# A two-layer hybrid trunk: branch A's norm writes each tile in one piece into places of its own, and the first head's preparation is begun ten steps sooner

## The chip, the cores and the metric

The kernel runs on one core of one Trainium2 chip. Its time is the device time of one execution in microseconds. Five engines work side by side: TensorE (PE; its weight loads are listed as PEld), VectorE (DVE), ScalarE (ACT), GpSimd (POOL) and SyncE (SP). SyncE issues every DMA of this kernel, in the order of its one instruction stream. Each engine works through its own instructions in order and waits where an instruction needs another engine's result or a buffer that is not free yet.

## The reference

Two layers of a decoder trunk on 1024 positions of width 1024. In each layer an RMS norm, one combined input product, three token mixers, a gated sum of their projections, an output product and a residual. The parts that the change touches are the norm of mixer A and the first head of mixer B:

```
a = a_val * sigmoid(a_glu)
a = causal_dwconv(a, a_dw) + a_dw_b            # 31 taps, 512 channels
a = layernorm(a, a_ln_g, a_ln_b)
y_a = silu(a) * silu(a_z)
...
q, k, v = split(silu(causal_dwconv(qkv, b_conv)))  # 8 heads of 128
kk = einsum("bhnid,bhnjd->bhnij", k, k)            # chunks of 64
a_mat = eye(c) + beta * kk * gamma_strict
sol = triangular_solve(a_mat, [v*beta, k*beta*exp(gc)], lower, unit_diagonal)
```

## The kernel before, in words

In a layer the products with the input weights come in two stages. In the first, blocks of weights are taken in pairs: seven products for eight (the names A11, S2, A12, S1, S3, A22, S4 are the seven weight operands of a pair, A and S in the rows). Each of the seven has four steps of three matmuls 128x512 (L357), so a pair has 28 steps. A product is summed in one of four PSUM buffers `ps`; ScalarE copies it out (L369) or VectorE adds it to the outputs (L373, L376). Weights (`wr`, L223) are combined on POOL and split in two parts on ScalarE and POOL (L184, L185). The outputs `o` are q, k, v (with a short convolution: start L715, taps L695 on VectorE, end L717), gates `g` (activation L726) and others, stored to DRAM by L729. In the second stage (L281, then L257) single products run, and beside them the eight heads of mixer B, one after the other.

Side work is woven into the first stage by step numbers counted from the start of a pair: `interleave` runs a side generator's next piece at step so and so, with a gap. The table of such numbers stands at lines 41 to 48; `S_HEAD = -4, 1` puts the first head's preparation four steps ahead of the third-last pair. TensorE's and VectorE's orders follow the code as written; a scheduler lays out ScalarE, POOL and SyncE, by priorities and readiness.

Two side generators matter here.

*The norm of mixer A* (`a_norm`, L1087 to L1102). The convolution's result lies in four units `acc`, one per 128 channels, channels on partitions. For each of eight tiles of 128 positions, `to_norm` transposes four 128x128 blocks into one PSUM buffer `pa` (L1115), takes mean and variance (`ln_stats`: VectorE L1076, L1078, L1080, POOL L1082 for the power, VectorE L1084), and writes the normalised tile back over the four blocks in `acc` by four activations 128x128 (L1118). Two rounds later the same four blocks are transposed again into a `pa` (L1097) and four activations apply gain, offset and Silu (L1100). There are two `pa` buffers.

*The first head* (`first_head`, L1403): load of k, q and the decay exponents (L736, L753: `gam`), the decay matrix (`head_decay`: select on POOL L789, exponentials on ScalarE L794), the keys (transposes L762, copies L777 and sums of squares L780, L891), the products of keys and queries (L811, L830, on VectorE L812 to L833), then small 16x16 blocks of the triangular matrix, which go to DRAM and come back regrouped (L847, L852), a solve on VectorE in 15 steps (`head_sub`: L862, L864, L865), its result stored in four pieces (L872) and fetched regrouped (L879), and later, with the second head under way, the inverse (`head_inv`: VectorE transpose L918, TensorE L923, L930). The second head's preparation follows at the end of the first stage (`S_NEXT`, `second_head`); its decay load is an L753 too.

The units are 4 KB tiles per partition in a ring of 24; `U(name)` takes one and `F` gives it back.

Of the kernel before, what the change touches and what calls it, by code (L numbers as in the profile page):

```python
# [11 lines left out]
AF = mybir.ActivationFunctionType  # L12
# [3 lines left out]
P = 128  # L16
T = 1024
D = 1024
NT = 8
# [24 lines left out]
S_C_MIX = 14, 6  # L44
S_SCALARS = 5, 12
S_A_NORM = 8, 5
S_HEAD = -4, 1
S_NEXT = 50, 61, 77, 76, 74
STEP_US, IDLE_US, WIDE_US = 0.7, 1.5, 1.4
EXTRA = 2  # L50
# [20 lines left out]
def hybrid_trunk_kernel(ctx: ExitStack, tc: tile.TileContext, x, norm_g, w_in, a_dw, a_dw_b,  # L71
# [4 lines left out]
    pe, act, pool, sp = nc.tensor, nc.scalar, nc.gpsimd, nc.sync  # L76
# [28 lines left out]
    def U(name, dt=F32):  # L105
        ring = free.popleft()
        t = ring.tile([P, 1024], dt, name=name)
        held[id(t)] = (ring, t)
        return t

    def F(*ts):
        for t in ts:
            free.append(held.pop(id(t))[0])
# [16 lines left out]
    ident = const.tile([P, P], F32, name="ident")  # L130
# [618 lines left out]
    def head_load(s, names):  # L749
        for nm in names:  # L750
            if nm == "d":
                s.gam = U("gam")
                sp.dma_start(out=by_chunk(s.gam), in_=gc_d[:, s.hd, :].partition_broadcast(P))  # L753
                continue
            assert nm == "z" or (s.layer, "qkv".index(nm) * 8 + s.hd) in saved
            s.u[nm] = fetch({"k": k_d, "q": q_d, "v": v_d, "z": z_d}[nm][s.hd], nm + "T")
        yield
# [7 lines left out]
    hsl = [slice(h * HALF, (h + 1) * HALF) for h in range(2)]  # L765
# [308 lines left out]
    def ln_stats(tp):  # L1074
        bs = sm.tile([P, 6], F32, name="bs")
        dve.bn_stats(bs, tp)  # L1076
        mv = sm.tile([P, 2], F32, name="mv")
        dve.bn_aggr(mv, bs)  # L1078
        ve = sm.tile([P, 1], F32, name="ve")
        dve.tensor_scalar(out=ve, in0=mv[:, 1:2], scalar1=EPS, scalar2=None, op0=ALU.add)  # L1080
        rs = sm.tile([P, 1], F32, name="lrs")
        pool.tensor_tensor(out=rs, in0=ve, in1=mhalf[:, 0:1], op=ALU.pow)  # L1082
        nm = sm.tile([P, 1], F32, name="nm")
        dve.scalar_tensor_tensor(out=nm, in0=mv[:, 0:1], scalar=-1.0, in1=rs, op0=ALU.mult, op1=ALU.mult)  # L1084
        return rs, nm

    def a_norm(l, accs):  # L1087


        for t in range(NT + 2):  # L1090
            if t < NT:
                to_norm(accs, t)
            if t >= 2:
                ts = slice((t - 2) * P, (t - 1) * P)
                tb = pa.tile([P, HALF], F32, name="pa")
                for c in range(4):
                    pe.transpose(tb[:, c * P:(c + 1) * P], accs[c][:, ts], ident)  # L1097
                for c in range(4):
                    gc, b_ = cols["alg", l] + c, cols["alb", l] + c
                    act.activation(out=accs[c][:, ts], in_=tb[:, c * P:(c + 1) * P], func=AF.Silu,  # L1100
                                   scale=vec[:, gc:gc + 1], bias=vec[:, b_:b_ + 1])
            yield  # L1102

    def split_units(src, name):
# [2 lines left out]
        F(src)  # L1107
        return hi, lo

    def to_norm(us, t):  # L1110

        ts = slice(t * P, (t + 1) * P)
        tp = pa.tile([P, HALF], F32, name="pa")
        for c in range(4):
            pe.transpose(tp[:, c * P:(c + 1) * P], us[c][:, ts], ident)  # L1115
        rs, nm = ln_stats(tp)
        for c in range(4):
            act.activation(out=us[c][:, ts], in_=tp[:, c * P:(c + 1) * P], func=AF.Identity, scale=rs, bias=nm)  # L1118

    def c_norm(gvs):  # L1120
        for t in range(NT):
            to_norm(gvs, t)
            yield
# [167 lines left out]
    def layer(l, before, ws=None, parts=1):  # L1291
# [131 lines left out]
        def at_step(nm, d, gap):  # L1423
            return at[nm] * 28 + d, gap
# [5 lines left out]
                    (late(lambda: gate_scalars(l, r)), *at_step("scalars", *S_SCALARS)),  # L1430
                    (late(fetch_a), *at_step("a_norm", 0, 1)),
                    (late(lambda: a_norm(l, accs)), *at_step("a_norm", *S_A_NORM)),
                    (late(first_head), *at_step("head", *S_HEAD)),
                    (late(lambda: head_load(hs[1], "k")), *at_step("head", S_NEXT[0], 1)),
# [98 lines left out]
    def late(f):  # L1533
        yield from f()
# [73 lines left out]
```

## Time and profile before

| | |
|---|---|
| median of 3 runs | 2663.96 us (2663.27 to 2668.45) |
| profiled execution | 2663.31 us, of it a span of 2661.5 us |
| mean granted TensorE clock | 0.991 |
| busy TensorE / VectorE / ScalarE / POOL | 2568.4 / 1656.7 / 1256.4 / 1423.5 us |

The profile is of one execution. [...] "Wait" is the idle time in front of an instruction with the event that ended it. Layer 0's norm of mixer A lies at 520 to 570 us, its first head's solve at 678 to 694 us; the same places of layer 1 are some 1312 us later.

### The profile page before, as it was taken

The numbers are of one execution on the slowest core, as the hardware profiler recorded it, in microseconds if no ns is written. First come the engines' busy times: TensorE is split into PE (matmuls) and PEld (weight loads), VectorE is DVE, ScalarE is ACT, GpSimd is POOL, SyncE is SP. The second block draws the span as 40 slices with busy tenths as digits, with TensorE's granted clock in tenths as the row PEclk, the third lists the DMA queues.
The fourth block names the chain that finished last, engine by engine and source line by source line (L and its number), as shares of the span: only waits on it lengthen the run. The fifth ranks groups of instructions, "written<-read, shape, count | busy, mean of one in ns | idle before, by whom it ended". The sixth has DMA issues, their size and how long they took to land.

```text
span 2661.5 us, 42685 instructions
## 1 busy us (share of the span) xinstructions
PE 2568.4 (97%) x15963; PEld 2113.4 (79%) x15963; DVE 1656.7 (62%) x2934; ACT 1256.4 (47%) x2996; POOL 1423.5 (53%) x1144
## 2 busy tenths in 40 slices
PE   7899999999899999999999999999998999999998
PEld 6688888778688888788867888887787888877887
DVE  6698999756445454445276889997564545444442
ACT  4434434565466666322134343356554666652221
POOL 7867777768433332363167777776673333324520
PEclk9999999999999999999999999999999999999999
DMA  4122333534634445554312223343445444445432
GB/s 158 48 64 88 104 95 107 155 108 122 184 103 111 145 106 169 182 170 138 107 68 63 63 82 110 95 150 104 118 131 173 114 131 112 136 139 189 156 130 76
DMA packets 361636, 319.65 MB, mean 120 GB/s; under 512 B 98931, under 2 KB 313557, under 8 KB 360405
## 3 DMA queue, kind: packets, MB, share of 16 engines
q1 hardware_dynamic: 361428, 316.92, 39.5%
q8 instruction: 126, 2.06, 0.3%
q14 instruction: 82, 0.66, 0.1%
HBM read 221.12 MB, written 95.75 MB: 119 GB/s over the span
## 4 chain that ended last, share of the span: by engine, by line
PE 80%; DVE 6%; POOL 4%; ACT 4%; DMA 3%; issue 2%; SPq 0%; DVEq 0%; POOLq 0%; ACTq 0%
PE ps L357 36%; PE ps L257 24%; PE ps L1271 7%; DMA gam<-gc_d 2%; PE pa L762 1%; PE ps L281 1%; POOL S L185 1%; PE pr L1012 1%; PE pr L1004 1%; PE pr L995 1%; POOL st L298 1%; PE pr L1021 1%; DMA wr<-in_w_in_dram 1%; PE pa L811 1%; DVE nm L1084 1%
## 5 line engine op out<-in xcount | busy, mean ns | idle before, releaser
L185 POOL TENSOR_TENSOR S<-st,S 128x512 fp32r<-128x512 f32 x248 | 332.5, 1341 | 166.1 <-ACT S L184 165.7
L695 DVE SCALAR_TENSOR_TENSOR pr<-o,dwT,pr 128x512 f32<-128x512 f32 (+7 forms) x480 | 357.0, 745 | 10.6
L357 PE MATMUL ps<-hT,A 128*128 128x512 f32 x1488 | 363.5, 392 | 0.0
L185 POOL TENSOR_TENSOR wl<-wr,wh 128x512 fp32r<-128x512 f32 (+2 forms) x164 | 198.6, 1225 | 293.1 <-PE ps L257 138.7
L257 PE MATMUL ps<-hT,wh 128*128 128x512 f32 x960 | 334.4, 429 | 0.0
L373 DVE TENSOR_TENSOR o<-o,ps 128x512 f32<-128x512 f32 x430 | 286.2, 681 | 77.4 <-PE ps L357 66.2
L357 PEld LDWEIGHTS ps<-hT,A 128*128 128x128 f32 x1488 | 279.4, 189 | 58.5 <-issue 0.5
L184 ACT ACTIVATE S<-st 128x512 fp32r<-128x512 f32 x248 | 156.7, 632 | 338.3 <-PE ps L357 196.4
L185 POOL TENSOR_TENSOR A<-wr,A 128x512 fp32r<-128x512 f32 x186 | 253.0, 1361 | 22.3 <-ACT A L184 22.0
L695 DVE SCALAR_TENSOR_TENSOR pr<-o,cvT,pr 128x512 f32<-128x512 f32 (+3 forms) x288 | 213.1, 752 | 48.9 <-ACT pr L715 43.3
L257 PE MATMUL ps<-hT,wl 128*128 128x512 f32 x480 | 189.3, 394 | 0.0
L184 ACT ACTIVATE A<-wr 128x512 fp32r<-128x512 f32 x186 | 117.2, 630 | 143.6 <-PE ps L357 126.3
L357 PE MATMUL ps<-T,A 128*128 128x512 f32 x744 | 183.4, 393 | 0.9 <-POOL A L185 0.5
L357 PE MATMUL ps<-hT,S 128*128 128x512 f32 x744 | 183.7, 392 | 0.0
L357 PE MATMUL ps<-T2h,S 128*128 128x512 f32 x496 | 167.9, 396 | 5.7 <-ACT T2h L184 3.0
L357 PE MATMUL ps<-T3h,S 128*128 128x512 f32 x496 | 167.1, 395 | 4.1 <-ACT o L369 3.6
L357 PE MATMUL ps<-T1h,S 128*128 128x512 f32 x496 | 164.7, 391 | 0.0
L357 PEld LDWEIGHTS ps<-T,A 128*128 128x128 f32 x744 | 139.1, 189 | 31.3 <-ACT o L717 1.6
L184 ACT ACTIVATE wh<-wr 128x512 fp32r<-128x512 f32 (+2 forms) x164 | 85.6, 549 | 165.2 <-issue 123.5
L357 PEld LDWEIGHTS ps<-hT,S 128*128 128x128 f32 x744 | 138.1, 188 | 28.4 <-ACT o L717 0.7
L257 PEld LDWEIGHTS ps<-hT,wh 128*128 128x128 f32 x960 | 151.1, 190 | 11.6
L1271 PE MATMUL ps<-woh,mg 128*128 128x512 f32 x512 | 140.7, 391 | 0.0
(298 smaller groups left out, 5723.6 us busy)
## 6 DMA issues: line engine op xcount, KB each, us to landing
wr<-in_w_in_dram SPq DMA_DIRECT2D x160, 512.0 KB
g_d<-gth SPq DMA_DIRECT2D x32, 512.0 KB
g_d<-o SPq DMA_DIRECT2D x16, 512.0 KB
z_d<-o SPq DMA_DIRECT2D x16, 512.0 KB
v_d<-o SPq DMA_DIRECT2D x16, 512.0 KB
k_d<-o SPq DMA_DIRECT2D x16, 512.0 KB
q_d<-o SPq DMA_DIRECT2D x16, 512.0 KB
gam<-gc_d SPq DMA_DIRECT2D x16, 512.0 KB
```

The source lines that it names most:

```text
L184: act.activation(out=hi, in_=src, func=AF.Copy)
L185: lo_eng.tensor_tensor(out=lo, in0=src, in1=hi.bitcast(F32), op=ALU.subtract)
L257: pe.matmul(ps[h], lhsT=w[wi][:, k, :], rhs=rhs(h, ri, k), start=(k == 0 and i == 0), stop=(k == kt - 1 and i == 2))
L281: pe.matmul(ps[h][:, sl], lhsT=w[wi][:, k, :], rhs=rhs(h, ri, k)[:, sl], start=(k == 0 and i == 0), stop=(k == kt - 1 and i == 2))
L298: eng.tensor_tensor(out=out, in0=in0, in1=in1, op=ALU.subtract)
L357: pe.matmul(ps, lhsT=wt[:, wi, k, :], rhs=blk(nb, ri, k), start=(k == 0 and i == 0), stop=(k == 3 and i == 2))
L373: dve.tensor_tensor(out=out, in0=other, in1=ps, op=ALU.add)
L695: dve.scalar_tensor_tensor(out=acc[:, lo:], in0=x[:, h * HALF + lo - s:(h + 1) * HALF - s], scalar=taps[s - 1], in1=acc[:, lo:], op0=ALU.m ...
L762: pe.transpose(tp[:, j * P:(j + 1) * P], src[:, half * 4 + j, :], ident)
L811: pe.matmul(tp[:, j], lhsT=kT[:, n], rhs=qT[:, n], start=True, stop=True)
L995: pe.matmul(ks, lhsT=kT[:, n], rhs=st, start=True, stop=True)
L1271: pe.matmul(ps[h], lhsT=mg[hh, ri, k // 4][:, k % 4, off:off + P], rhs=wo[k][wi][:, h * HALF:(h + 1) * HALF], start=(k == 0 and i == 0), s ...
```

## The change

In `a_norm` two units `an` are taken; each is cut in two halves, which gives four places of 128 positions by 512 channels. `to_norm` writes tile t by one activation 128x512 into place t mod 4, and the second transposes read that place. Mixer C's norm calls `to_norm` without a place and keeps its four activations. `S_HEAD` goes from −4 to −14. In the changed kernel the new activation is L1122, the second transposes are L1099, the Silu is L1102, and lines behind are shifted.

```diff
--- before.py
+++ after.py
@@ -44,7 +44,7 @@
 S_C_MIX = 14, 6
 S_SCALARS = 5, 12
 S_A_NORM = 8, 5
-S_HEAD = -4, 1
+S_HEAD = -14, 1
 S_NEXT = 50, 61, 77, 76, 74
 STEP_US, IDLE_US, WIDE_US = 0.7, 1.5, 1.4
 EXTRA = 2
@@ -1087,18 +1087,22 @@
     def a_norm(l, accs):
 
 
+        both_ways = U("an"), U("an")
+        place = [u[:, sl] for sl in hsl for u in both_ways]
         for t in range(NT + 2):
             if t < NT:
-                to_norm(accs, t)
+                to_norm(accs, t, place[t % 4])
             if t >= 2:
                 ts = slice((t - 2) * P, (t - 1) * P)
                 tb = pa.tile([P, HALF], F32, name="pa")
                 for c in range(4):
-                    pe.transpose(tb[:, c * P:(c + 1) * P], accs[c][:, ts], ident)
+                    pe.transpose(tb[:, c * P:(c + 1) * P], place[(t - 2) % 4][:, c * P:(c + 1) * P], ident)
                 for c in range(4):
                     gc, b_ = cols["alg", l] + c, cols["alb", l] + c
                     act.activation(out=accs[c][:, ts], in_=tb[:, c * P:(c + 1) * P], func=AF.Silu,
                                    scale=vec[:, gc:gc + 1], bias=vec[:, b_:b_ + 1])
+            if t == NT + 1:
+                F(*both_ways)
             yield
 
     def split_units(src, name):
@@ -1107,13 +1111,16 @@
         F(src)
         return hi, lo
 
-    def to_norm(us, t):
+    def to_norm(us, t, place=None):
 
         ts = slice(t * P, (t + 1) * P)
         tp = pa.tile([P, HALF], F32, name="pa")
         for c in range(4):
             pe.transpose(tp[:, c * P:(c + 1) * P], us[c][:, ts], ident)
         rs, nm = ln_stats(tp)
+        if place is not None:
+            act.activation(out=place, in_=tp, func=AF.Identity, scale=rs, bias=nm)
+            return
         for c in range(4):
             act.activation(out=us[c][:, ts], in_=tp[:, c * P:(c + 1) * P], func=AF.Identity, scale=rs, bias=nm)
```

On ScalarE, at the first tiles of the norm in layer 0 (`an` is the new place, S and A are weight splits, `o` and `pr` a convolution). Before:

```order
L184 ACTIVATE S_4581<-st 128x512
L1118 ACTIVATE acc<-pa,nm,lrs 128x128 x8
L717 ACTIVATE o_4281<-pr 128x512
L1100 ACTIVATE acc<-pa,vec 128x128 x4
L184 ACTIVATE A_4631<-wr 128x512
L1118 ACTIVATE acc<-pa,nm,lrs 128x128 x4
L184 ACTIVATE S_4677<-st 128x512
L1100 ACTIVATE acc<-pa,vec 128x128 x4
L1118 ACTIVATE acc<-pa,nm,lrs 128x128 x4
L184 ACTIVATE S_4695<-st 128x512
```

After:

```order
L184 ACTIVATE S_4577<-st 128x512
L1122 ACTIVATE an<-pa,nm,lrs 128x512 x2
L1102 ACTIVATE acc<-pa,vec 128x128 x4
L717 ACTIVATE o_4281<-pr 128x512
L184 ACTIVATE A_4624<-wr 128x512
L1122 ACTIVATE an<-pa,nm,lrs 128x512
L184 ACTIVATE S_4667<-st 128x512
L1102 ACTIVATE acc<-pa,vec 128x128 x4
L1122 ACTIVATE an<-pa,nm,lrs 128x512
L184 ACTIVATE S_4685<-st 128x512
```

Eight narrow activations became two wide ones, and the two groups of four behind them one wide one each; the first Silu group now stands ahead of an L717 instead of behind it. Further on in the norm, at the tile whose four stood as three, then an L369 and a split, and then one, there is one L1122 now.

On VectorE, in front of the first head's solve (`o` are outputs of the second-last pair of blocks, `sub` is the solve's unit). Before:

```order
L373 TENSOR_TENSOR o_5824<-o_5823,ps 128x512
L373 TENSOR_TENSOR o_5823<-o_5823,ps 128x512
L373 TENSOR_TENSOR o_5823<-o_5824,ps 128x512
L862 MEMSET sub 128x16
L864 TENSOR_TENSOR sub<-sub 128x8x2
L865 TENSOR_REDUCE sub<-sub 128x8
L373 TENSOR_TENSOR o_5824<-o_5823,ps 128x512
L373 TENSOR_TENSOR o_5824<-o_5824,ps 128x512
L864 TENSOR_TENSOR sub<-sub 128x8x3
L865 TENSOR_REDUCE sub<-sub 128x8
L864 TENSOR_TENSOR sub<-sub 128x8x4
L865 TENSOR_REDUCE sub<-sub 128x8
```

After:

```order
L373 TENSOR_TENSOR o_5571<-o_5570,ps 128x512
L373 TENSOR_TENSOR o_5571<-o_5571,ps 128x512 x2
L373 TENSOR_TENSOR o_5570<-o_5570,ps 128x512
L373 TENSOR_TENSOR o_5810<-o_5809,ps 128x512
L862 MEMSET sub 128x16
L864 TENSOR_TENSOR sub<-sub 128x8x2
L865 TENSOR_REDUCE sub<-sub 128x8
L864 TENSOR_TENSOR sub<-sub 128x8x3
L865 TENSOR_REDUCE sub<-sub 128x8
L864 TENSOR_TENSOR sub<-sub 128x8x4
L865 TENSOR_REDUCE sub<-sub 128x8
L373 TENSOR_TENSOR o_5809<-o_5809,ps 128x512
```

The solve begins two sums L373 earlier in its pair, and fewer of the sums stand among its first steps.

On SyncE, behind the solve (`s_0_155` is the solve's scratch in DRAM; the first `gam` and kT, qT belong to the second head). Before:

```order
L729 DMA g_d<-o_5824 128x1024
L753 DMA gam<-gc_d 128x8x128
L736 DMA kT<-k_d 128x1024
L736 DMA qT<-q_d 128x1024
L729 DMA g_d<-o_5823 128x1024
L736 DMA qT<-q_d 128x1024
L223 DMA wr<-in_w_in_dram 128x8x128 x2
L566 DMA hT<-b_d 128x2048 x2
L872 DMA s_0_155<-sub 32x8x16 x4
L736 DMA vT<-v_d 128x1024
L753 DMA gam<-gc_d 128x8x128
```

After:

```order
L223 DMA wr<-in_w_in_dram 128x8x128
L872 DMA s_0_155<-sub 32x8x16 x4
L729 DMA g_d<-o_5810 128x1024
L753 DMA gam<-gc_d 128x8x128
L879 DMA sub<-s_0_155 128x8x32
L729 DMA g_d<-o_5809 128x1024
L736 DMA qT<-q_d 128x1024
L736 DMA kT<-k_d 128x1024
L736 DMA qT<-q_d 128x1024
L223 DMA wr<-in_w_in_dram 128x8x128
L566 DMA hT<-b_d 128x2048 x2
L223 DMA wr<-in_w_in_dram 128x8x128
```

The solve's four stores (L872) went from behind loads of weights and of `hT` to the front of the pair's gate store and of the second head's decay load, and its fetch (L879), which before stood behind a further weight load and store (out of the piece shown), now follows that decay load.

## Rows read from the trace of the kernel before

**Rows 1.** The page: busy time of each engine, share of the span, instructions.

```profile
PE 2568.4 (97%) x15963; PEld 2113.4 (79%) x15963; DVE 1656.7 (62%) x2934; ACT 1256.4 (47%) x2996; POOL 1423.5 (53%) x1144
```

**Rows 2.** TensorE's waits: releaser, us in total, times, longest.

```profile
PE pa L1097 <- ACT acc L1118: 11.4, 8, 2.9
```

**Rows 3.** Timeline of TensorE, norm of layer 0: start, us, work, [wait before].

```profile
531.03 0.66 PE L1097 MATMUL pa<-ident,acc 128*128 128x128 f32 x4 [2.90 <-ACT acc L1118]
...
540.76 0.66 PE L1097 MATMUL pa<-ident,acc 128*128 128x128 f32 x4 [0.68 <-ACT acc L1118]
...
547.01 0.66 PE L1097 MATMUL pa<-ident,acc 128*128 128x128 f32 x4 [1.73 <-ACT acc L1118]
```

**Rows 4.** Timeline of TensorE, first head of layer 0.

```profile
701.10 0.50 PE L357 MATMUL ps<-T3h,S 128*128 128x512 f32 x1 [1.71 <-ACT o L369]
...
724.62 1.08 PE L923 MATMUL pr<-sub 32*32 32x32 f32 x64 [5.51 <-DVE sub L918]
```

**Rows 5.** Timeline of TensorE, first head of layer 1.

```profile
2016.57 0.50 PE L357 MATMUL ps<-T3h,S 128*128 128x512 f32 x1 [1.89 <-ACT o L369]
...
2039.11 1.08 PE L923 MATMUL pr<-sub 32*32 32x32 f32 x64 [4.58 <-DVE sub L918]
```

**Rows 6.** Chain of waits, 680 to 727 us: start, us, what.

```profile
687.58 11.03 DMA gam<-gc_d
...
717.13 6.96 DMA sub<-s
```

**Rows 7.** Stretches: us, busy (instructions) by engine, TensorE clock, DMA share, GB/s.

```profile
531.00:536.00 5.00, 4.97 (x28) 4.08 (x28) 3.16 (x8) 4.42 (x11) 1.85 (x2) 1.00 0.26 107
725.00:731.00 6.00, 6.00 (x128) 4.69 (x121) 0.43 (x2) 2.05 (x6) 0.54 (x3) 0.52 0.45 112
1843.00:1849.00 6.00, 5.72 (x21) 4.71 (x22) 3.11 (x7) 4.15 (x11) 1.84 (x2) 0.72 0.22 90
2016.00:2021.00 5.00, 4.43 (x12) 3.53 (x13) 1.59 (x3) 4.32 (x12) 2.96 (x3) 0.66 1.07 359
2038.00:2045.00 7.00, 5.89 (x139) 4.62 (x140) 0.45 (x1) 2.05 (x6) 1.51 (x2) 0.51 0.50 126
```

**Rows 8.** Timeline of ScalarE, norm of layer 0.

```profile
529.47 1.51 ACT L1118 ACTIVATE acc<-pa,nm,lrs 128x128 f32<-128x128 f32 x4 [2.05 <-DVE nm L1084]
...
544.44 1.16 ACT L1118 ACTIVATE acc<-pa,nm,lrs 128x128 f32<-128x128 f32 x3 [0.59 <-DVE nm L1084]
...
546.49 0.47 ACT L1118 ACTIVATE acc<-pa,nm,lrs 128x128 f32<-128x128 f32 x1
```

**Rows 9.** ScalarE by line and shape: busy us, mean ns of one, idle before.

```profile
L777 ACT ACTIVATE kE<-pa 128x512 f32<-128x512 f32 x32 | 19.0, 593 | 9.3 <-PE pa L762 9.3
...
L1066 ACT ACTIVATE pr<-o,vec,dwT 128x512 f32<-128x512 f32 x16 | 12.4, 780 | 1.9 <-DVE o L1333 1.5
```

**Rows 10.** Timeline of POOL, norm of layer 0.

```profile
528.69 0.55 POOL L1082 TENSOR_TENSOR lrs<-ve,mhalf 128x1 f32<-128x1 f32 x1
```

**Rows 11.** Timeline of TensorE, behind the norm of layer 0.

```profile
618.31 1.86 PE L357 MATMUL ps<-T,A 128*128 128x512 f32 x7 [0.21 <-ACT o L717]
```

**Rows 12.** Chain of waits, 550 to 622 us.

```profile
575.25 10.39 DMA gam<-gc_d
```

**Rows 13.** Timeline of VectorE, the solve of layer 0.

```profile
672.29 0.69 DVE L373 TENSOR_TENSOR o<-o,ps 128x512 f32<-128x512 f32 x1 [4.39 <-ACT A L184]
...
677.67 0.69 DVE L373 TENSOR_TENSOR o<-o,ps 128x512 f32<-128x512 f32 x1 [2.03 <-PE ps L357]
...
693.36 0.29 DVE L865 TENSOR_REDUCE sub<-sub 128x8 f32<-128x128 f32 x1
...
717.30 1.12 DVE L833 SCALAR_TENSOR_TENSOR gam<-pa,Wn,gam 128x128 f32<-128x128 f32 x4 [0.20 <-PE pa L830]
```

**Rows 14.** Timeline of SyncE's issues, layer 0.

```profile
705.13 2.44 SPq L872 DMA_DIRECT2D s<-sub  x4
```

**Rows 15.** Timeline of ScalarE, first head of layer 0.

```profile
703.22 0.58 ACT L369 ACTIVATE o<-ps 128x512 f32<-128x512 f32 x1
```

## Prediction

> **What bounds the kernel now.** I read the page's first part first. TensorE is busy for 2568.4 of 2661.5 us, far above every other engine [rows 1]. So little over 90 us of TensorE idle time is all that an edit of this kind can take, beside the time in which TensorE runs at less than its full clock; an edit to another engine is worth what it takes out of a TensorE wait. Second, TensorE's waits by line: the branch A norm's second transposes, L1097, wait eight times for the normalising activations L1118, 11.4 us in all [rows 2]. Third, the two stretches that the change touches. In the norm of layer 0, TensorE waits 2.90, 0.68 and 1.73 us at L1097 [rows 3]; the fourth wait there is what is left of half the 11.4 us, 0.4. At the other place the largest single wait is L923, the first matmul of head 0's inverse: 5.51 us in layer 0 [rows 4], 4.58 in layer 1 [rows 5]. The chain of waits says what stands behind it: a fetch of 6.96 us that SyncE issued at 717.13 [rows 6]. Last, the granted clock behind these waits: 0.52 and 0.51 behind L923, 0.66 behind a wait of 1.89 us for an L369 in layer 1, and behind the norm's 2.90 us 1.00 in layer 0 but 0.72 in layer 1 [rows 7]. A wait can therefore cost twice, once as idle time and once as clock.
>
> **The norm (both layers alike).** Four L1118 on 128x128 took 1.51 us together [rows 8]. They become one L1122 on 128x512. The trace has no activation of that shape that reads PSUM with a per-partition scale and bias; the nearest are the 128x512 copy out of PSUM (L777, 593 ns) and the 128x512 Identity with scale and bias (L1066, 780 ns) [rows 9]. Between these ends I take 0.70 us, so 0.8 us less a tile, 0.7 to 0.9 by the ends.
>
> [...]
>
> What does this shorten? In both kernels the transposes L1097 of tile t use one of two PSUM buffers, and it comes free when the activations of tile t+1 have read it. So the activation's end releases TensorE, and the place that it writes matters less. The first wait also has the statistics in front of it: the POOL power L1082 begins only at 528.69, behind an L298 [rows 10], and the activation waits for the vector operation that follows it [rows 8]. Nothing in the change moves that, so 2.90 becomes 2.1. The 0.68 goes. The 1.73 is one in which ScalarE ran three of the four, then an L369 and a weight split, and the fourth 2 us later [rows 8]; one operation can't be divided so, and it goes too, and so does the last 0.4. The order on ScalarE now puts the fifth tile's activation behind an L717 and a split; I charge 0.4 for that. Per layer: 0.8 + 0.7 + 1.7 + 0.4 − 0.4 = 3.2 us. Of this some is given back. At 618.31 TensorE already waits 0.21 us for branch B's convolution, whose chain comes from head 0's decay fetch (10.39 us from 575.25) [rows 11, 12]. The activations in front of that fetch stand in a new order too: one that sends a store ahead of it now comes behind a split of some 0.6 us. If TensorE arrives 3.2 us sooner there and the chain does not, it waits longer; but the chain itself hangs on TensorE's products further back. I charge 0.8, leaving 2.35 per layer, 4.7 for both. Layer 1 can also regain the clock: 6.00 us at 0.72 against 1.00 [rows 7] is 1.7 at most, and I take 1.5, since the wait left is shorter than the one without a drop in layer 0. The norm: 6.2 us, with 1.8 (the narrowing alone at the first wait, twice 0.9) and 9 as its ends.
>
> The new places cost nothing: their four tiles are units of the same ring that hold branch B's data long stored by then, and no product reads them.
>
> **The first head.** Ten steps earlier moves its transposes and products on TensorE by ten steps of three matmuls each, its solve on VectorE, and its DMAs on SyncE. The work is the same. What changes is the time at which the solve ends, and with it the chain solve, store L872, fetch L879, transpose L918, L923.
>
> Before, the solve begins behind the sum L373 of 677.67, and its last reduction ends at 693.36 + 0.29 = 693.65 [rows 13]. The four stores are issued only at 705.13 [rows 14], because SyncE has weights and reloads in front of them, and the fetch at 717.13. Now the solve stands behind the sum of 672.29 [rows 13], two L373 earlier, which is 5.4 us. It keeps its own length, and one L373 that stood within it now follows it, so it ends near 687. The stores come directly behind it, and head 1's decay fetch and the solve's own fetch directly behind these. Even at 691 plus some 11 us (the slowest fetch near it took 11.03) plus 7, the data is there by 709. TensorE reaches L923 at 724.62 − 5.51 = 719.11. The fetch is hidden, and the 5.51 us wait on it goes.
>
> What is late next? Three things. (1) VectorE: L833 has to end before L918; it ends now at 717.30 + 1.12 = 718.4 [rows 13], plus 0.45 for the transpose and 0.5 to L923 makes 719.6 with the delay below. (2) Head 1's decay fetch. It was issued at 687.58 and landed 11.03 later [rows 6]. Now its place on SyncE is behind the four stores, so behind the solve's end, and behind a store whose sum is ended by the solve: I get 1.7 us later. ScalarE's exponentials on it (L794) come before the L369 of 703.22 [rows 15]; that L369 ended at 703.80. With all eight exponentials now in a row, but without the L369 and the split that stood among them, it ends about 0.45 later (0.2 to 1.2). The 1.71 us wait at 701.10 for the L369 that stood among them goes [rows 4], as it now runs ahead of them, but the products behind the later one then wait up to 2.4 us. That is one wait for another. (3) The keys' activations and the sums of squares behind them release L830 as before, 0.45 later.
>
> So L923 stands at about 719.6 instead of 724.62: 5.0 us in layer 0. In layer 1 the wait is 4.58, and less the same 0.5 it gives 4.1. Then the clock: 6.00 us at 0.52 is 2.9 us lost at most [rows 7]; a third of that stretch is two groups of 64 small matmuls (1.08 us for the L923 group [rows 4]) that may not follow the clock, so I take 2.0; in layer 1, 5.89 busy at 0.51 likewise, 1.9. The head: 5.0 + 4.1 + 2.0 + 1.9 = 13.0, with 4 (2 of each wait, no clock) and 17 as its ends.
>
> **The sum.** 6.2 + 13.0 = 19.2. Against it: the waits that stay or arise (2.1 in each norm, 2.4 in each layer before the last products) can lower the clock as the 1.89 us in layer 1 did (0.66 over 5 us, 1.7 at most [rows 7]). I charge two of these four, 3 us. That leaves 16.2, and 2663.3 (the profiled execution) − 16.2 = 2647.1. The median shown, 2663.96, is 0.7 higher; I stay with 2647.
>
> [...]
>
> **The rivals.**
> - *The head alone.* The norm's four waits are released by the statistics and by what lies between on ScalarE rather than by the activation's length. For it: the activation of the first tile waited 2.05 us for VectorE [rows 8]. Against it: 1.51 us of the 2.90 are the activations themselves. Gain 13 less some 2 of clock: 2652.
> - *The norm alone.* Head 1's decay fetch, pushed behind the solve's stores, takes the wait over: what L923 gained is waited for before the last products. For it: its 11.03 us lie on the chain already [rows 6], and 1 us of delay costs 1 us there. Against it: I find 1.7 us later issue, of which ScalarE's new order absorbs most. 6.2 plus nothing: 2657.
> - *No change.* The solve does not begin sooner, because the keys' preparation hangs on head 0's loads; and in the norm TensorE reaches each convolution wait sooner and stands there. For it: SyncE and VectorE are in order. Against it: the sums' order is fixed and they end by TensorE's clock. 2663.
> - *Slower.* The stores, now in front of head 1's decay fetch on the one queue, hold it: if the solve still ended at 693.65, that fetch would be issued some 7.7 us later than at 687.58, and L369, the keys and L830 with it; L923 would stand at 727, 2.4 later in each layer, with the clock as low as before. It decides from a solve end of about 692 on (a delay beyond 6.7 us). With the norm giving nothing: 2668.
>
> **How the numbers follow.** Chances: forecast 0.55 (own range 2640 to 2653), the head alone 0.15, the norm alone 0.17, no change 0.08, slower 0.05. The lower end: all waits and the clock's drops gone would be 9 + 17 = 26, 2637, and I take 2638. The upper end takes in the norm alone, 2657, and a us more; the two cases above it hold 0.13, and some of the forecast's own tail lies below 2638. Within 0.2% means within 5.3 us, which is about what a measurement of this kernel can tell. Faster than 2658: the first two, and nearly three quarters of the third, 0.82; same 0.13; slower 0.05.
>
> **What would show it.** Right: L1122 of 0.6 to 0.8 us; waits at the second transposes near 2.1 and then under 0.5; the solve's last reduction near 687; the fetch of the solve issued near 691 instead of 717; L918 following L833 and no DMA in front of it; the clock behind L923 at 1.00. Wrong: an L923 that still waits for a fetch; a wait of more than 3 us for L369 before the last products or for L777's keys; the time lost at 618 as a wait of 2 us or more for L717.

## The result and the profile after

The changed kernel took 2652.24 us (median of 4 runs, 2648.29 to 2653.49), the kernel before 2664.23 (4 runs): 12.0 us faster by the medians. The ratio is 0.995 with a 95% interval of 0.9938 to 0.9961, which is 13.3 us. The forecast was 2647, with a range of 2638 to 2658. The profiled execution took 2653.15 us, with a span of 2651.4. A second set of runs on another occasion gave 2651.56, at a ratio of 0.9949 (0.9936 to 0.9961).

TensorE's waits by line (releaser, us in total, times, longest), of the changed kernel:

```profile
PE ps L357 <- ACT o L369: 11.6, 6, 4.8
...
PE pa L1099 <- ACT an L1122: 5.0, 2, 2.5
```

The norm's eight waits of 11.4 us [rows 2] are two of 5.0. L923 no longer waits for a fetch. But the waits of the pairs' products for L369 are 11.6 us in all, with one of 4.8. In the kernel before they were 6.3:

```profile
PE ps L357 <- ACT o L369: 6.3, 6, 1.9
```

In time, TensorE at the norm and at the first head of layer 0, the same head in layer 1, and the first wait behind each norm, of the changed kernel:

```profile
530.02 0.66 PE L1099 MATMUL pa<-ident,an 128*128 128x128 f32 x4 [2.50 <-ACT an L1122]
...
614.18 2.96 PE L357 MATMUL ps<-T,A 128*128 128x512 f32 x12 [0.22 <-ACT o L717]
...
702.81 1.50 PE L357 MATMUL ps<-hT,S 128*128 128x512 f32 x3 [4.82 <-ACT o L369]
...
717.94 0.75 PE L923 MATMUL pr<-sub 32*32 32x32 f32 x64
...
721.78 0.75 PE L930 MATMUL pr<-sub 32*32 32x32 f32 x64 [1.05 <-ACT sub L925]
...
731.52 1.14 PE L968 MATMUL pr<-sub,gam 64*64 64x64 f32 x16 [1.15 <-POOL sub L964]
...
1924.83 2.97 PE L357 MATMUL ps<-T,A 128*128 128x512 f32 x12 [0.26 <-ACT o L717]
...
2012.68 0.96 PE L357 MATMUL ps<-hT,S 128*128 128x512 f32 x3 [4.05 <-ACT o L369]
...
2027.84 0.75 PE L923 MATMUL pr<-sub 32*32 32x32 f32 x64
```

Read these against the kernel before as distances. At the convolution's wait, 618.31 before [rows 11] and 614.18 now, TensorE is 4.13 us ahead. The statistics' power on POOL in front of the norm began at 528.69 [rows 10] and now begins at 528.41, so 0.28 of it was there already: **the norm of layer 0 gave 3.85 us**. At L923 it is 724.62 [rows 4] against 717.94, 6.68 ahead: **the head gave 2.55 us up to there**, not 5.0. In layer 1 the wait behind the norm went from 1933.22 (the row below, of the kernel before) to 1924.83, 8.39 ahead, and L923 from 2039.11 [rows 5] to 2027.84, 11.27 ahead: 2.9 us from the head, where 4.1 was forecast, with a new wait of 4.05 for an L369.

```profile
1933.22 2.06 PE L357 MATMUL ps<-T,A 128*128 128x512 f32 x8 [0.24 <-ACT o L717]
```

What stood in the head's way is on VectorE, POOL, SyncE and ScalarE of the changed kernel. First VectorE, from the sum in front of the solve to the sums behind it, then POOL in the same time:

```profile
668.17 0.69 DVE L373 TENSOR_TENSOR o<-o,ps 128x512 f32<-128x512 f32 x1 [4.81 <-PE ps L357]
668.82 0.07 DVE L862 MEMSET sub<- 128x16 f32 x1
...
671.92 0.93 DVE L864 TENSOR_TENSOR sub<-sub 128x48 f32<-128x48 f32 x1
...
673.13 0.98 DVE L864 TENSOR_TENSOR sub<-sub 128x56 f32<-128x56 f32 x1
...
674.39 1.10 DVE L864 TENSOR_TENSOR sub<-sub 128x64 f32<-128x64 f32 x1
...
685.31 0.29 DVE L865 TENSOR_REDUCE sub<-sub 128x8 f32<-128x128 f32 x1
685.52 1.28 DVE L373 TENSOR_TENSOR o<-o,ps 128x512 f32<-128x512 f32 x2
```

```profile
671.49 1.30 POOL L185 TENSOR_TENSOR A<-wr,A 128x512 fp32r<-128x512 f32 x1
672.75 1.28 POOL L185 TENSOR_TENSOR S<-st,S 128x512 fp32r<-128x512 f32 x1
674.11 1.29 POOL L298 TENSOR_TENSOR st<-st,wr 128x512 f32<-128x512 f32 x1
```

The solve begins where the forecast put it (668.82, which is 672.95 on the clock of the kernel before, 4.13 later). It ends at 685.60, or 689.7 on that clock, where 687 was forecast. Its multiplications L864 of 128x48 to 128x64 take 0.93 to 1.10 us, and four more, up to 128x96, 0.95 to 1.28. In the kernel before the solve has slow ones too, but fewer: four of 1.01 to 1.07 and two of 0.43 and 0.58. There 128x48 is slow and 128x56 and 128x64 take 0.25 and 0.27:

```profile
684.18 1.06 DVE L864 TENSOR_TENSOR sub<-sub 128x48 f32<-128x48 f32 x1
...
686.51 0.27 DVE L864 TENSOR_TENSOR sub<-sub 128x64 f32<-128x64 f32 x1
```

In the changed kernel's rows each slow one ends about 0.1 us behind a POOL operation: 672.85 behind 672.79, 674.11 behind 674.03, 675.49 behind 675.40. Two sums L373 stand behind the solve's last reduction and end at 686.80. Now SyncE's issues and ScalarE, again of the changed kernel:

```profile
672.81 0.38 SPq L223 DMA_DIRECT2D wr<-in_w_in_dram  x1
685.63 1.80 SPq L872 DMA_DIRECT2D s<-sub  x4
687.53 0.39 SPq L729 DMA_DIRECT2D g_d<-o  x1
688.02 1.32 SPq L753 DMA_DIRECT2D gam<-gc_d  x1
690.12 0.37 SPq L879 DMA_DIRECT2D sub<-s  x1
```

```profile
699.83 2.45 ACT L794 ACTIVATE gam<-gam,ng 128x128 f32<-128x128 f32 x8 [6.32 <-POOL gam L789]
702.18 0.57 ACT L369 ACTIVATE o<-ps 128x512 f32<-128x512 f32 x1
```

Between the weight load of 672.81 and the stores L872, SyncE issues nothing: it stands 12.4 us at L872 until the solve's last reduction, with all later DMAs behind it. In the kernel before it waited 0.2 us there. The second head's decay load goes out at 688.02, which is 692.15 on the clock of before: 4.6 us later than its 687.58 [rows 6], where 1.7 was forecast. The exponentials start 4.1 later and the L369 behind them ends 3.1 later (702.75 against 703.80, with 4.13 between the clocks), where 0.45 was forecast. TensorE is ready for the last product of the pairs at 697.99 and stands until 702.81.

The stretches with a lowered clock (us, busy by engine, granted clock as a share of the full one, DMA share, GB/s):

```profile
703.00:707.00 4.00, 4.00 (x15) 3.17 (x15) 3.76 (x5) 1.40 (x3) 3.64 (x4) 0.57 1.08 410
717.00:721.00 4.00, 3.73 (x80) 2.61 (x78) 0.70 (x3) 3.44 (x13) 1.09 (x1) 1.00 0.81 274
734.00:741.00 7.00, 7.00 (x29) 5.68 (x28) 0.00 (x0) 1.61 (x4) 0.00 (x0) 0.53 0.62 186
1838.00:1844.00 6.00, 5.66 (x21) 4.54 (x22) 3.78 (x9) 3.47 (x8) 1.83 (x2) 0.72 0.23 90
2013.00:2017.00 4.00, 4.00 (x16) 3.34 (x15) 3.76 (x5) 1.27 (x3) 3.65 (x4) 0.59 1.09 418
```

Behind L923 the clock is 1.00 now (before: 0.52 [rows 7]). But it is 0.57 over the 4 us behind the new 4.82 us wait (0.59 behind the 4.05 of layer 1), and 0.53 for 7 us from 734 on, behind the waits of L930 and L968; the norm of layer 1 still ends in 0.72. So at the first product L1004 of layer 0, behind the head, TensorE is 3.75 us ahead (740.50 against 744.25 before), less than the 4.13 with which it came to the head: in this execution nothing of the head's gain in layer 0 is left, the clock included.

Which wait a drop follows changes from one execution to the next. In this profile the twelve products L357 that soon follow the norm's first wait take 2.91 us in layer 0, at a clock of 1.00, and 4.49 in layer 1, at 0.62, behind a wait of 2.50 us each. In the second profile of the changed kernel the same twelve take 3.44 us in layer 0, behind 2.50, and 2.89 in layer 1, behind 2.51.

### The profile page after: what moved, and what is told of

Same layout as the page of the kernel before. It is cut to its first block, busy times and chain, and to the rows that moved or that the text cites. A ratio compares the mean times of both kernels' runs of the same rounds, so it can differ in the third digit from the quotient of the medians.

```text
span 2651.4 us, 42619 instructions
## 1 busy us (share of the span) xinstructions
PE 2567.0 (97%) x15963; PEld 2114.7 (80%) x15963; DVE 1655.0 (62%) x2934; ACT 1242.7 (47%) x2948; POOL 1419.5 (54%) x1144
## 4 chain that ended last, share of the span: by engine, by line
PE 79%; DVE 8%; POOL 5%; DMA 3%; issue 3%; ACT 2%; SPq 0%; DVEq 0%; POOLq 0%; ACTq 0%
PE ps L357 35%; PE ps L257 24%; PE ps L1278 7%; PE pa L762 1%; POOL S L185 1%; DVE sub L864 1%; DMA wr<-in_w_in_dram 1%; POOL st L298 1%; DMA g_d<-o 1%; PE pr L995 1%; PE pr L1004 1%; PE pr L1012 1%; DMA gam<-gc_d 1%; PE pr L1021 1%; PE ps L281 1%
## 5 line engine op out<-in xcount | busy, mean ns | idle before, releaser
L357 PE MATMUL ps<-hT,A 128*128 128x512 f32 x1488 | 364.8, 392 | 0.0
L257 PE MATMUL ps<-hT,wh 128*128 128x512 f32 x960 | 336.2, 431 | 0.0
L373 DVE TENSOR_TENSOR o<-o,ps 128x512 f32<-128x512 f32 x430 | 286.1, 681 | 75.8 <-PE ps L357 73.5
L357 PEld LDWEIGHTS ps<-hT,A 128*128 128x128 f32 x1488 | 279.4, 189 | 58.2 <-issue 0.5
L357 PE MATMUL ps<-hT,S 128*128 128x512 f32 x744 | 185.1, 395 | 8.9 <-ACT o L369 8.9
L257 PE MATMUL ps<-hT,wl 128*128 128x512 f32 x480 | 190.5, 397 | 0.0
L357 PE MATMUL ps<-T,A 128*128 128x512 f32 x744 | 183.3, 394 | 1.5 <-POOL A L185 1.1
L357 PE MATMUL ps<-T2h,S 128*128 128x512 f32 x496 | 167.9, 396 | 5.7 <-ACT T2h L184 3.0
L357 PEld LDWEIGHTS ps<-hT,S 128*128 128x128 f32 x744 | 139.6, 190 | 38.6 <-ACT o L369 9.7
L357 PE MATMUL ps<-T1h,S 128*128 128x512 f32 x496 | 165.7, 392 | 0.0
L357 PEld LDWEIGHTS ps<-T,A 128*128 128x128 f32 x744 | 139.9, 189 | 32.0 <-POOL A L185 1.9
L357 PE MATMUL ps<-T3h,S 128*128 128x512 f32 x496 | 165.4, 392 | 0.0
L257 PEld LDWEIGHTS ps<-hT,wh 128*128 128x128 f32 x960 | 152.2, 192 | 11.9
L309 POOL TENSOR_TENSOR st<-wr 128x512 f32<-128x512 f32 x62 | 83.7, 1349 | 110.4 <-DMA wr<-in_w_in_dram 99.4
```

The costliest lines, as they stand in the source:

```text
L257: pe.matmul(ps[h], lhsT=w[wi][:, k, :], rhs=rhs(h, ri, k), start=(k == 0 and i == 0), stop=(k == kt - 1 and i == 2))
L309: pool.tensor_tensor(out=s1, in0=a21, in1=a22, op=ALU.add)
L357: pe.matmul(ps, lhsT=wt[:, wi, k, :], rhs=blk(nb, ri, k), start=(k == 0 and i == 0), stop=(k == 3 and i == 2))
L373: dve.tensor_tensor(out=out, in0=other, in1=ps, op=ALU.add)
```

## The experiments

All were compared with the kernel before, whose median was 2665.63, 2665.51 and 2666.81 us in the three sets. The ratio's 95% interval stands in brackets.

**The norm alone.**

```diff
-S_HEAD = -14, 1
+S_HEAD = -4, 1
```

> The changed norm with the first head begun where it was before (S_HEAD -4). Theory A, read from the two traces: TensorE is ahead by 3.85 us behind the norm of layer 0 and by 3.94 us more behind that of layer 1, and nothing of it is given back, so 2664.2 - 7.8 = 2656.4, with L923 still waiting some 5 us in each layer. Rival B: part of it is only seen because the head was moved too; alone the norm's gain is waited for at the convolution or at the first head's fetch, and 2659 or more is left.

Measured 2657.47 us, 8.2 faster, 0.9969 (0.9956 to 0.9981). Theory A. TensorE's waits show it: the norm's are gone but for the first, L923 waits as before.

```profile
PE pr L923 <- DVE sub L918: 10.3, 2, 5.8
...
PE pa L1099 <- ACT an L1122: 5.0, 2, 2.5
```

**The head alone**, in the kernel before.

```diff
-S_HEAD = -4, 1
+S_HEAD = -14, 1
```

> The norm as before, the first head begun ten steps sooner (S_HEAD -14). Theory A (the two parts add): 12.0 - 7.8 = 4.2 us gained, 2660, with a new wait of 4 to 5 us for an L369 before the last product of the pairs in place of the wait at L923. Rival B (the parts help each other): 2664, nothing gained. Rival C (the norm's new order is what holds the head back): the forecast's 9 to 13 us, 2651 to 2655.

Measured 2660.54 us, 5.1 faster, 0.998 (0.9971 to 0.9988). Theory A again: 8.2 and 5.1 are together 13.3, what both gave by the ratio (12.0 by the medians). The waits have changed places, L923's for L369's:

```profile
PE ps L357 <- ACT o L369: 11.9, 6, 4.7
PE pa L1097 <- ACT acc L1118: 11.3, 8, 2.9
```

**Places, but four pieces.**

```diff
-            act.activation(out=place, in_=tp, func=AF.Identity, scale=rs, bias=nm)
+            for c in range(4):
+                act.activation(out=place[:, c * P:(c + 1) * P], in_=tp[:, c * P:(c + 1) * P], func=AF.Identity, scale=rs, bias=nm)
```

> The changed kernel (S_HEAD -14), but the normalised tile is written into its place by four activations 128x128 instead of one 128x512. Theory A: only the one piece counts, the place of its own nothing; waits at the second transposes as before (2.90, 0.68, 1.73, 0.40 a layer) and the time of the head's move alone, 2660. Rival B: half of the norm's gain comes from the places, 2656. Rival C: the places alone do it, 2652.

Measured 2662.92 us, 0.9987 (0.9978 to 0.9996): the head's share at most (its interval overlaps that of the head alone), nothing of the norm's. Theory A. Its waits at the second transposes are those of the kernel before to the tenth [rows 2]:

```profile
PE pa L1099 <- ACT an L1123: 11.4, 8, 2.9
```

The place of its own is only what allows the one piece.

**The second head's decay load sooner**, in the changed kernel.

```diff
-S_NEXT = 50, 61, 77, 76, 74
+S_NEXT = 50, 57, 77, 76, 74
```

> The changed kernel with the load of the second head's q and decay exponents at step 57 instead of 61, which puts the decay load L753 on SyncE ahead of the solve's four stores L872 and of the gate store, into a unit that is free sooner. Theory A: the forecast's mis-sized step is the decay load behind the stores and behind the sums that the solve delays; with it loaded sooner L794 runs early, the 4.82 and 4.05 us waits for L369 go and with them a drop of the clock, 2641 to 2645. Rival B: TensorE then meets the next late thing at once (keys' activations, the solve's fetch), less than half of it is kept, 2648 or more. Rival C: the load collides with the weight transfers and nothing changes, 2652.

Measured 2639.18 us, 0.9901 (0.9886 to 0.9916), 13 us below the changed kernel and just below theory A's window. The load now stands on SyncE ahead of the solve's stores. SyncE's issues, ScalarE, and TensorE's waits:

```profile
666.94 0.37 SPq L753 DMA_DIRECT2D gam<-gc_d  x1
...
683.40 1.81 SPq L872 DMA_DIRECT2D s<-sub  x4
```

```profile
678.55 2.46 ACT L794 ACTIVATE gam<-gam,ng 128x128 f32<-128x128 f32 x8 [8.34 <-POOL gam L789]
```

```profile
PE ps L357 <- ACT o L369: 2.7, 4, 0.7
```

The load leaves 21 us sooner, the exponentials run 21 us sooner, and the waits for L369 fall from 11.6 to 2.7. This shows that the long waits for L369 hang on the place of this load on SyncE, the step that the forecast had mis-sized. It does not price that error: the load goes far ahead of where the forecast had it, and most of the waits that the kernel before had for L369 go too. The second head's key load, which stood behind it, also goes out sooner (685.79 against 693.94), so not all of the 13 us need be the decay load's.

**The POOL product queued behind the copies**, in the changed kernel. L880, a multiplication with the mask `corner`, stood on POOL for the second head 5.06 us for that head's block store, with L963 and L964 of the first head, for which L968 waits, behind it.

```diff
-        pool.tensor_tensor(out=s.inv[:, 0:256].rearrange("p (n i) -> p n i", n=8), in0=bd, in1=bc(corner, 1, 8), op=ALU.mult)
+        s.bd = bd
+        if not last_z64:
+            set_corner(s)
...
     def head_inv(s):
...
+        if last_z64:
+            with tc.issue_after(last_z64[0].ins):
+                set_corner(s)
...
-        pool.tensor_copy(out=z64[32:64, :, 32:64], in_=zc[32:64])
+        last_z64[:] = [pool.tensor_copy(out=z64[32:64, :, 32:64], in_=zc[32:64])]
```

`set_corner` is the line taken out; `issue_after` puts it behind the named instruction in POOL's order.

> The changed kernel, but the POOL product L880 of the heads from the second on is queued behind the copies L963 and L964 of the head before it, instead of ahead of them. Theory A: L968's new wait of 1.15 us in layer 0 is L880 standing on POOL for the second head's block store, and the clock's drop at 734 to 741 us follows from it; without it 2648 to 2651. Rival B: the clock drops there whatever L968 does (the 4.82 us wait before it, or the 32x32 matmuls), only the wait itself goes, 2651 to 2652.

Measured 2649.79 us, 0.9939 (0.9927 to 0.9952); the changed kernel stands at 0.995 and 0.9949 in its two sets, so the 2 us are inside the intervals. The mechanism is there. POOL's rows of this kernel, with L972 and L973 for the copies and L910 for the product:

```profile
726.06 0.39 POOL L972 COPY sub<-sub 32x256 f32<-32x256 f32 x1
726.50 0.39 POOL L973 COPY sub<-sub 32x256 f32<-32x256 f32 x1
730.58 0.74 POOL L910 TENSOR_TENSOR sub<-sub,corner 128x256 f32<-128x256 f32 x1 [3.69 <-DMA s<-sub]
```

The copies no longer wait for the store, and L968's wait is gone. Whether the clock's drop at 734 followed from it is not shown. For it: the 16 matmuls L974 behind L968 (L983 here) and the two L257 behind them take 1.14 and 0.73 us here, against 1.80 (at 0.56) and 1.22 (at 0.50) in the changed kernel, and the second profile of the changed kernel has both again, a wait of 1.44 us at L968 and then 1.97 and 1.22. Against it: the head alone had a wait of 1.02 us at L968, and L974 behind it took 1.14.

**The load sooner, alone**, in the kernel before.

```diff
-S_NEXT = 50, 61, 77, 76, 74
+S_NEXT = 50, 57, 77, 76, 74
```

> The kernel before with only the second head's decay load at step 57 instead of 61. Theory A: the waits for L369 (1.71 and 1.89 us) go and with them the keys' lateness; SyncE's order puts the solve's stores ahead of the reloads hT too, so L923 comes some 7 us sooner a layer with a wait of 1 to 2 us left; 2650 to 2655. Rival B: L879 stays as late as 717 and L923 with it, nothing is gained, 2664.

Measured 2658.58 us, 0.9973 (0.9963 to 0.9982): between the two theories, so both missed. L923 did come 9.8 us sooner in layer 0 (714.78), more than theory A said. Half was lost again behind it: at L1004 (739.40) 4.85 us are left. TensorE's wait for POOL at L968, which the kernel before did not have, is 7.2 us in all:

```profile
PE pr L968 <- POOL sub L964: 7.2, 2, 4.0
```

**The norm and the load, the head as before**, in the changed kernel.

```diff
-S_HEAD = -14, 1
-S_NEXT = 50, 61, 77, 76, 74
+S_HEAD = -4, 1
+S_NEXT = 50, 57, 77, 76, 74
```

> The changed norm and the second head's decay load at step 57, but the first head begun where it was before (S_HEAD -4). Theory A: the head's ten steps are worth what L923 still waits for the solve's fetch, 1 to 2 us a layer and the clock behind it; 2642 to 2647 against 2639 with all three. Rival B: with the load sooner the head's move is worth nothing, 2639. Rival C: without the head's move the load gives nothing, 2656 as with the norm alone.

Measured 2648.2 us, 0.9935 (0.9922 to 0.9947). Above theory A's window, and not for its reason. L923 waits 1.45 us in layer 0 and not at all in layer 1; the 9 us to the run with norm, load and head are then lost largely at L968, as the next run shows. POOL of this run, and the clock behind L968 in both layers:

```profile
716.18 1.09 POOL L789 TENSOR_SCALAR_AFFINE_SELECT gam<-gam 128x1024 f32<-128x1024 f32 x1 [17.32 <-DMA gam<-gc_d]
...
724.93 0.72 POOL L880 TENSOR_TENSOR sub<-sub,corner 128x256 f32<-128x256 f32 x1 [1.17 <-DMA s<-sub]
725.59 0.39 POOL L963 COPY sub<-sub 32x256 f32<-32x256 f32 x1
```

```profile
726.00:737.00 11.00, 10.52 (x49) 8.49 (x50) 0.00 (x0) 2.15 (x4) 1.35 (x2) 0.53 0.60 138
2033.00:2044.00 11.00, 8.41 (x43) 6.80 (x44) 0.00 (x0) 2.15 (x4) 2.40 (x4) 0.53 0.51 122
```

POOL stands 17.32 us for the third head's decay load, then works off what has queued, stands for L880's store, and only then copies for L968. The two waits (2.77 and 4.10 us) are followed by 11 us at 0.53.

**The same with the POOL product queued behind the copies**: the last diff and the one of `set_corner` together.

> As the run with the norm and the sooner decay load but without the head's ten steps, and with the POOL product of the later heads (L880 there) queued behind the copies L963 and L964 of the head before it. Theory A: L968's waits of 2.77 and 4.10 us come from POOL's queue; of that queue this takes L880 with its wait, 1.9 us a layer, and the clock's drop behind L968 goes or shrinks: 2640 to 2645 against 2648. Rival B: the rest of the queue (the third head's select, which waited 17 us for its load, and what stands behind it) holds L963 all the same; 2646 to 2649. If it comes to 2639 or less, the head's move is worth nothing beside the other two.

Measured 2639.34 us, 0.9899 (0.9884 to 0.9914): faster than theory A said, and as fast as with the head's move.

```profile
726.00:737.00 11.00, 11.00 (x61) 9.18 (x62) 4.08 (x19) 5.52 (x17) 0.00 (x0) 1.00 0.67 162
2020.00:2038.00 18.00, 16.93 (x115) 12.82 (x115) 0.00 (x0) 4.02 (x9) 6.94 (x9) 0.53 0.50 120
```

```profile
PE pr L955 <- issue: 2.2, 1, 2.2
...
PE pr L977 <- POOL sub L973: 0.3, 1, 0.3
```

L977 (L968 there) waits 0.3 us in all, and in layer 0 the clock is whole. This shows L880's place on POOL to be worth 9 us where the head is late. The drop in layer 1 lies elsewhere; the last section comes back to it.

**All of it**: the changed kernel with the one line of `S_NEXT` and the diff of `set_corner`.

> The changed kernel with both: the second head's decay load at step 57 and the POOL product queued behind L963 and L964. Theory A: with the head begun ten steps sooner L968 does not wait any more (none is seen there in the run with the load alone), so the second edit gives nothing: 2637 to 2640 against 2639. Rival B: it still keeps POOL clear for the head, 2636 or less.

Measured 2638.67 us, 0.99 (0.9887 to 0.9914): theory A, no more than with the load alone. Three kernels stand at 2639: norm, load and head; norm, load and POOL product; all four. With the norm, the sooner load and the POOL product in place, the head's ten steps give nothing that can be measured; without the POOL product they are worth 9 us.

**The changed kernel again.**

> The changed kernel once more, on the chip of these comparisons: 2652, between 2648 and 2654.

Measured 2651.56, as expected.

## Why the prediction was right, and where it was not

- *The bound and the two places* held. TensorE's waits at the norm and at L923 were what the change took; longer waits for L369 are what it cost.
- *The norm's first wait.* L1122 took 0.78 us (the mean of the 16 is 781 ns), the upper end of the two rows taken as bounds. The wait is 2.50, not 2.1: the activation ended 0.7 sooner as forecast, but TensorE came to it 0.3 sooner, a small wait in front of it being gone.
- *The other three waits* went, 0.68, 1.73 and 0.4, as forecast. The charge of 0.4 for the fifth tile and that of 0.8 for what the convolution would take back were wrong: at 614.18 TensorE waits 0.22 where it waited 0.21 [rows 11]. That chain came forward with TensorE's own products, on which it hangs, as the prediction said and then charged for all the same. So 3.85 instead of 2.35 a layer; the clock in layer 1, put at 1.5, gave nothing in this execution (0.72 as before [rows 7]), and by the second profile that could as well have come out the other way. The norm: 6.2 forecast, 8.2 measured alone.
- *The head.* The step that failed is "It keeps its own length ... so it ends near 687", and "I get 1.7 us later" for the second head's decay load, which rests on it. The solve ended at 689.7 on that clock. Of the 2.7 us about 1.5 are its length (16.8 us against 15.3 from 678.32 to 693.65), with more slow multiplications in it; the other 1.2 are the sum L373 that the forecast took out of the solve, though four stand within it in either kernel. The sums behind it, the gate's activation and store, and the decay load on the same queue all moved with it, 4.6 us in all. So L923 gained 2.55 instead of 5.0 in layer 0 and 2.9 instead of 4.1 in layer 1, and in layer 0 the clock lost behind L369 (0.57) and from 734 on (0.53) what it regained at L923. The 64 matmuls of L923, of which the forecast said that they may not follow the clock, took 1.08 us at 0.50 before and 0.75 at 1.00 now. 13.0 forecast; 5.1 measured alone.
- *The rivals.* "The norm alone" named the mechanism, the decay load pushed behind the stores, and gave it 0.17. It was half true: the load took back about half of L923's gain, not all. The forecast said of it that ScalarE's new order would absorb most; it absorbed 1.0 of the 4.1 us by which the exponentials began later.
- *Late things behind L923* were missing. Of "What is late next" the list ended at L923; the waits of L930 (1.05 us, for an L925 queued on ScalarE behind L844) and L968 (1.15 us) are new.
- *The sum.* 16.2 forecast, 12.0 measured (13.3 by the ratio): the norm 2 more, the head 8 less, and the charge of 3 for clock drops that was put apart is in the measured parts. The time fell into the range by luck as much as by the sum: the norm's extra 2 and the charge of 3 made up for most of the head's 8.
- *Slips of the working.* 3.2 less 0.8 is 2.4, not 2.35. The pieces up to L923 (718.4, 0.45, 0.5 and the delay of 0.45) are 719.8, not 719.6. By the prediction's own 1.7 at a solve's end of 687, the slower rival's delay at 693.65 is 8.4, not 7.7. Together they move the forecast by half a us at most.

## What to carry to other kernels

When a step is begun sooner, follow every in-order queue that it enters past the point where its own wait goes: here the solve, once sooner, pushed two sums, a store and the next head's load, and moving that load four steps up was worth 13 us in the changed kernel, as much as the whole change, and 6.9 us in the kernel before. A moved step's length is not a constant (the solve took 15.3 us before and 16.8 now): look at what the other engines do in its new place. And if several waits in a row end at about the same time, removing one shows the next; price the change by the row of waits that is left, not by the first.

## What was not expected of the hardware

The multiplications L864, whose two operands both lie in the unit `sub`, took 0.93 to 1.28 us in the changed kernel's solve (0.43 to 1.07 in that of the kernel before) where a POOL operation on 128x512 was running when they began, and ended about 0.1 us or less behind it; the others took 0.18 to 0.38. (The one of 671.44 began 0.09 us ahead of such an end and took 0.22.) The reductions L865 between them took 0.17 to 0.29 us and the sums L373, with an operand in `ps`, 0.68 or 0.69, two of them 1.27 or 1.28, also while POOL was at work. That POOL's operation is what lengthened the multiplications is not shown: no run here took POOL's work away.

In the run with the norm, the load and the POOL product, TensorE stood 2.17 us in the middle of L955's 32 matmuls, for nothing that the profile shows, and the clock was 0.53 for 18 us from there on. The run with the norm and the load had 1.21 us at the same place in layer 1, also for nothing that is shown. What stopped it stays open.
